# A hybrid encoder layer: the divided front weights are kept in DRAM by the first half and loaded by the second

## Chip, cores and metric

The kernel runs on one core of a Trainium2 chip. The metric is the device time of one execution in microseconds (us), given as the median of several runs. A profiled execution gives the trace; its engines are called PE (matmul), PEld (weight load for PE), DVE (vector), ACT (scalar), POOL (gpsimd) and SP (which issues DMA transfers).

## What is computed

One layer on 1024 tokens of width 1024, all in float32:

```python
p = x @ w_in[l]                                   # one projection, 43 blocks of 128 columns
y_fox  = _forgetting_attention(q, k, v, f_logit + fox_f_bias[l])
y_rwkv = _rwkv7_time_mix(r_r, r_k, r_v, ...)
merged = (sigmoid(gate_fox) * (y_fox @ p_fox[l]) + sigmoid(gate_rwkv) * (y_rwkv @ p_rwkv[l]))
x = _layer_norm(DN_ALPHA * x + merged @ w_o[l], ...)
x = _layer_norm(DN_ALPHA * x + _peer(x, peer_w_q[l], sub_keys, u, v), ...)
```

`_peer` takes, for each token, 128 experts out of 16384 (top-k over scores), a dot product with each expert's row of u, and a weighted sum of their rows of v.

## The kernel before, in words

**Exact float32 products from halves.** PE multiplies float32r operands here, so every operand is divided into a high half (a cast on ACT, line 290) and a low half (source minus high, a subtraction on POOL or DVE, line 291); `mm3` (line 283) then makes three matmuls: high by high, high by low, low by high. This holds for the activations and for the weights.

**The front, in two halves.** The tokens are processed in two halves of 512 (`PARTS`). Each half runs the forgetting attention (`fox`), the RWKV part (`rwkv_half`), the merge, the output projection with its layer norm (`merge_half`), and the query projection with its scores (`queries`). Each half reads the same list of weight tiles, 128x1024 float32 (512 KB in DRAM): 9 for the attention, 30 for RWKV and the gates, 8 for the merge, 12 for the output projection (four of them twice), 16 for the queries: 75 tiles per half, 71 different ones, 150 loads in all. `Weights` (line 294) hands them out in that order. `get` gives the pair (wh, wl) of the tile that PE is about to use. `ahead`, called just after the first matmuls of that tile, divides the next tile (ACT cast, then the subtraction, by DVE for every eighth tile and by POOL otherwise) and has SP load the raw tile after that. There are two raw buffers and two pairs. Most tiles feed 24 matmuls of 512 columns; those of the second half of the output's columns (`W_OUT` 4 to 7, each read twice) feed 12.

**Background work.** While PE goes through the front, a second stream of work is mixed in: `topk` (DVE) on the scores of finished tokens, then `experts_in`: POOL issues 128 gathers per token tile (`DMA_INDIRECT g<-u,eidx`, line 1399, 128 rows of 4 KB each), and DVE makes one dot product per gather (`CUSTOM_DVE_ANT_0 g<-g,ext`, line 1405, 1024 elements). It begins when the first half's scores are there, so it runs through the second half of the front and on into the dense block. Every matmul recorded by `mm` (line 272) gives the background some microseconds of credit, so where its steps stand among the front's depends on the matmuls alone.

**Order.** PE's order is that of the code. The orders of ACT, DVE, POOL and SP come from the framework's scheduler, which plays the program through with its own durations; each engine then takes its instructions strictly in that order. A gather on POOL waits for a free place (DVE has read it); a low half on POOL waits for the cast, which waits until PE has left the pair's buffer. SP takes its transfers in order as well: one whose buffer is not free holds up what stands behind it.

**The dense block.** After both halves, from about 1866 us, three token tiles go through all 16384 experts by matmul, and the other five by gathers of u and v.

Of the kernel before, what the change touches and what calls it, by code (L numbers as in the profile page):

```python
# [10 lines left out]
F32 = mybir.dt.float32  # L11
F32R = mybir.dt.float32r
# [35 lines left out]
LOMOD = 8  # L48
# [10 lines left out]
PARTS = [(0, 512), (512, 512)]  # L59
# [12 lines left out]
N_W = W_Q + 16  # L72
# [49 lines left out]
class Filler:  # L122


    def __init__(self):
        self.q = []
        self.debt = 0.0
# [161 lines left out]
def split(g, hi, lo, src, lo_eng=None):  # L289
    g.act.copy(hi, src)  # L290
    (lo_eng or g.dve).tensor_sub(lo, src, hi.bitcast(F32))  # L291


class Weights:


    def __init__(self, g, order):
        self.g, self.order = g, list(order)
        self.raw, self.hl = {}, {}
        self.nl = self.ns = self.n = 0  # L300
        self._load()

    def _load(self):
        if self.nl < len(self.order):
            g = self.g
            raw = g.wp.tile([128, 1024], F32, name="wraw", bufs=g.nraw)
            g.sp.dma_start(raw, g.A["w"][self.order[self.nl]])
            self.raw[self.nl] = raw
            self.nl += 1

    def _split(self):
        if self.ns < len(self.order):
            g = self.g
# [5 lines left out]
            self._load()  # L319

    def get(self, i):
        assert self.order[self.n] == i, (self.n, self.order[self.n], i)
        if self.ns <= self.n:
            self._split()
        r = self.hl.pop(self.n)
        self.n += 1
        return r

    def ahead(self):
        if self.ns <= self.n:  # L330
            self._split()


def proj_gen(g, ps, wi, x, c0, w=None, ahead=True):
# [23 lines left out]
def xload(g, hf, then=None):  # L358

    t0, n = PARTS[hf]  # L360
    g.xs = ExitStack()
    xp = g.xs.enter_context(g.tc.tile_pool(name="xp", bufs=1, side="right"))
    xh = xp.tile([128, 8, n], F32R, name="xh")
    xl = xp.tile([128, 8, n], F32R, name="xl")
    with g.tc.tile_pool(name="xr", bufs=4, side="right") as rp:
        for k in range(8):
            raw = rp.tile([128, n], F32, name="xraw")
            g.sp.dma_start(raw, g.A["xt"][k, :, t0:t0 + n])
            split(g, xh[:, k, :], xl[:, k, :], raw, g.pool if k % 3 == 2 else g.dve)
            if k == 0 and then:  # L370
                then()
    g.X = xh, xl


def body(ctx, g):
    tc, nc, A = g.tc, g.nc, g.A
    dve, act, pool, sp = g.dve, g.act, g.pool, g.sp
    cst = ctx.enter_context(tc.tile_pool(name="cst", bufs=1))
    g.lo_mod, g.nraw = LOMOD, 2
# [7 lines left out]
    def dram(name, shape, dt=F32):  # L387
        return nc.dram_tensor(name, shape, dt, kind="Internal").ap()
# [5 lines left out]
    g.gtd = [dram(f"gtd{p}", (16, 128, n)) for p, (_, n) in enumerate(PARTS)]  # L394
    g.x1d = [dram(f"x1d{t}", (128, D)) for t in range(8)]
    g.scd = [dram(f"scd{t}", (128, 2048)) for t in range(8)]
    g.cd = dram("cd", (128 * len(DENSE) // BLK, 128, 128 - HALF, BLK))
    g.yd = [dram(f"yd{t}", (128, D)) for t in range(8)]
    g.seld = [dram(f"seld{t}", (128, 128), I32) for t in range(8)]
# [23 lines left out]
    order, half = [], [FOX_F] + [FOX_QK + i for i in range(8)]  # L423
# [15 lines left out]
        order += half[:nh]  # L439
    with ExitStack() as fe:  # L440
        g.X = None
        front_setup(g, fe, order)
        for hf, (t0, n) in enumerate(PARTS):
            g.t0, g.n, g.cols = t0, n, slice(t0, t0 + n)
            with ExitStack() as hx:
                hp = hx.enter_context(tc.tile_pool(name="hp", bufs=1))
                kt = hp.tile([128, 4, n], F32, name="kt")
                more = [hp.tile([128, D], F32, name=f"g{i}") for i in range(KRING[1] if hf else 0)]
                g.keys.add(more)
                if g.X is None:  # L450
                    xload(g, hf)
                g.B.rate = RATEP[0]
                fox(g, hf, g.X)
                g.B.rate = RATEP[1]
                yr = rwkv_half(g, hf, g.X, kt) if g.stop != "fox" else None
                g.xs.close()
                g.X = None
                g.B.rate = RATEP[2]
                if g.stop not in ("fox", "rwkv"):
                    merge_half(g, hf, yr)  # L460
                g.keys.drop(more)
                g.B.busy = True
                while any(a is p for a in g.keys.alive.values() for p in more):
                    g.B._step()
                g.B.busy = False
# [20 lines left out]
def front_setup(g, fe, order):  # L486
    tc, nc, A = g.tc, g.nc, g.A
    dve, act, sp = g.dve, g.act, g.sp
    fp = fe.enter_context(tc.tile_pool(name="fe", bufs=1))
    g.wp = fe.enter_context(tc.tile_pool(name="wp", bufs=2))  # L490
    g.W = Weights(g, order)
    xload(g, 0, g.W._split)
    tab = fp.tile([128, TAB.shape[1]], F32, name="tab")
    sp.dma_start(tab, A["tab"])

    def tb(name, rows=slice(0, 128)):
        o, n = TAB_OFF[name]
        return tab[rows, o:o + n]

    g.tb = tb  # L500
    g.rst = fp.tile([128, 512], BF16, name="rst")
# [16 lines left out]
    dve.memset(g.ccar, 0.0)  # L518

def fox(g, hf, X):
# [1340 lines left out]
```

## Time and profile before

| | |
|---|---|
| median of 3 runs | 3679.65 us (3674.41 to 3681.93) |
| profiled execution, own time | 3699.46 us |
| its span from first to last instruction | 3697.7 us |
| busy: PE, DVE, POOL, ACT | 87%, 64%, 61%, 33% of the span |
| mean granted PE clock | 0.918 |
| moved by DMA | 1019 MB, mean 276 GB/s |
| casts wh and subtractions wl | 150 on ACT; 131 on POOL, 19 on DVE |
| stages (by their matmuls) | first half 6.7 to 778 us, second half 778 to 1866 us, dense block 1866 to 3698 us |

The profile's windows give the busy time of each engine in a stretch of time; its groups give the same per kind of instruction, with the idle time before them and what ended it; its waits name pairs of waiting and awaited instructions with their total time. A wait matters where it is PE's, or that of an engine for which PE waits.

### The profile page before, as it was taken

Reading aid. Unit: us, or ns where it says so; the run is one execution under the profiler, and the core shown is the slowest. Engines: PE = TensorE matmul, PEld = TensorE weight load, DVE = VectorE, ACT = ScalarE, POOL = GpSimd, SP = SyncE. Lnnn points to the kernel's source line nnn. Section 1 sums busy time; section 2 is a strip of 40 time slices with the busy share of each in tenths; the row PEclk is TensorE's granted clock in tenths of the full one; section 3 lists DMA queues with packets and bytes.
Section 4 is the critical chain, followed back from the end, with each engine's and each line's share of the span. In section 5 each row is a group of like instructions: output and inputs, shape, how many; then the busy total and the mean of one; then the engine's idle time right before and its main releaser. Section 6 shows DMA issues by size and latency. Waiting matters only on the chain. (4 is left out here: it accounts for less than half of the span.)

```text
span 3697.7 us, 55476 instructions
## 1 busy us (share of the span) xinstructions
PE 3229.0 (87%) x20656; PEld 2343.4 (63%) x20656; DVE 2367.7 (64%) x5127; ACT 1237.3 (33%) x2528; POOL 2261.5 (61%) x1752
## 2 busy tenths in 40 slices
PE   7899999989987778777867767899999999999997
PEld 5577777775565566556633322677777777776665
DVE  3235423458888998799758965577666767774324
ACT  3443222333443221222234433333333333333332
POOL 2031115426676666577845566788887888886773
PEclk9899999998988877789978889999999999999998
DMA  4121133548777777877979989999999999999995
GB/s 141 52 91 45 44 115 117 194 135 291 250 266 248 243 238 261 283 243 263 316 273 363 355 334 366 357 363 360 381 382 382 402 392 393 394 387 340 378 391 198
DMA packets 338127, 1019.35 MB, mean 276 GB/s; under 512 B 46272, under 2 KB 84928, under 8 KB 336064
## 3 DMA queue, kind: packets, MB, share of 16 engines
q0 software_dynamic: 184320, 671.17, 49.2%
q1 hardware_dynamic: 141424, 323.85, 25.0%
q10 hardware_dynamic: 12112, 20.78, 1.5%
q8 instruction: 162, 2.65, 0.3%
q14 instruction: 109, 0.89, 0.1%
HBM read 960.55 MB, written 55.12 MB: 275 GB/s over the span
## 5 line engine op out<-in xcount | busy, mean ns | idle before, releaser
L1399 POOL DMA_INDIRECT g<-u,eidx x566 | 720.0, 1272 | 350.4 <-issue 94.2
L1405 DVE CUSTOM_DVE_ANT_0 g<-g,ext 128x1024 f32<-128x1024 f32 x566 | 775.6, 1383 | 44.1 <-DMA g<-u,eidx 43.3
L291 POOL TENSOR_TENSOR wl<-wraw,wh 128x1024 fp32r<-128x1024 f32 x131 | 320.6, 2447 | 491.4 <-ACT wh L290 464.2
L1701 POOL DMA_INDIRECT vr<-v,ve x434 | 459.9, 1060 | 212.5 <-issue 106.3
L273 PE MATMUL pg<-vr,win 128*32 128x512 f32 x1736 | 314.1, 637 | 64.6 <-DMA vr<-v,ve 57.7
L273 PE MATMUL b<-xh,uh 128*128 128x384 f32 x1024 | 349.7, 341 | 13.3 <-DVE C L1586 12.1
L273 PE MATMUL b<-xh,ul 128*128 128x384 f32 x1024 | 351.1, 343 | 5.7 <-POOL ul L291 4.6
L273 PE MATMUL b<-xl,uh 128*128 128x384 f32 x1024 | 348.4, 340 | 0.0
L290 ACT CAST wh<-wraw 128x1024 fp32r<-128x1024 f32 x150 | 157.3, 1048 | 498.4 <-PE pj L273 266.0
L273 PE MATMUL v<-vl,ch 128*128 128x512 f32 x768 | 305.9, 398 | 14.0 <-POOL vl L291 13.9
L273 PE MATMUL pj<-xh,wh 128*128 128x512 f32 x624 | 291.2, 467 | 22.7 <-DVE ql L556 11.1
L273 PE MATMUL v<-vh,ch 128*128 128x512 f32 x768 | 303.1, 395 | 0.0
L273 PE MATMUL v<-vh,cl 128*128 128x512 f32 x768 | 301.7, 393 | 0.0
L290 ACT CAST uh<-uraw 128x512 fp32r<-128x512 f32 x256 | 158.5, 621 | 360.5 <-PE b L273 253.6
L273 PE MATMUL pj<-xh,wl 128*128 128x512 f32 x624 | 264.2, 423 | 5.3 <-POOL wl L291 4.1
L1701 POOL DMA_INDIRECT C<-v,ve x206 | 216.0, 1048 | 84.3 <-issue 50.0
L273 PE MATMUL pj<-xl,wh 128*128 128x512 f32 x624 | 265.0, 425 | 2.3 <-DVE xl L291 2.3
L291 DVE TENSOR_TENSOR vl<-vraw,vh 128x512 fp32r<-128x512 f32 x128 | 134.7, 1052 | 182.0 <-ACT vh L290 114.3
L290 ACT CAST vh<-vraw 128x512 fp32r<-128x512 f32 x256 | 158.1, 620 | 252.6 <-PE v L273 166.1
L273 PEld LDWEIGHTS v<-ab 128*128 128x128 f32 x768 | 114.0, 220 | 180.9 <-issue 112.4
L291 POOL TENSOR_TENSOR ul<-uraw,uh 128x512 fp32r<-128x512 f32 x128 | 171.9, 1343 | 87.3 <-ACT uh L290 71.4
L273 PEld LDWEIGHTS b<-xh,uh 128*128 128x128 f32 x1024 | 193.6, 189 | 35.1 <-DVE C L1586 16.5
(357 smaller groups left out, 6865.6 us busy)
## 6 DMA issues: line engine op xcount, KB each, us to landing
wraw<-w SPq DMA_DIRECT2D x150, 512.0 KB
uraw<-ut SPq DMA_DIRECT2D x128, 512.0 KB
vraw<-vt SPq DMA_DIRECT2D x128, 512.0 KB
cd<-S SPq DMA_DIRECT2D x12, 1344.0 KB
C<-cd SPq DMA_DIRECT2D x63, 256.0 KB
g<-u,eidx POOLq DMA_INDIRECT x566
gtd<-tmp ACTq DMA_DIRECT2D x32, 256.0 KB
g<-gtd SPq DMA_DIRECT2D x32, 256.0 KB
```

Source lines behind the costliest of these rows:

```text
L273: g.pe.matmul(o, l, r, start=start, stop=stop_)
L290: g.act.copy(hi, src)
L291: (lo_eng or g.dve).tensor_sub(lo, src, hi.bitcast(F32))
L1399: pool.indirect_dma_start(out=place, out_offset=None, in_=A["u"], in_offset=bass.IndirectOffsetOnAxis(ap=idx[:, n:n + 1], axis=0))
L1405: dve.tensor_tensor_reduce(out=gg, in0=gg, in1=xt, scale=1.0, scalar=0.0, op0=OP.mult, op1=OP.add, accum_out=hh[:, k:k + 1])
L1701: g.pool.indirect_dma_start(out=place, out_offset=None, in_=g.A["v"], in_offset=bass.IndirectOffsetOnAxis(ap=self.meta[i][1][:, t:t + 1], ...
```

## The change

The first half divides its 75 tiles as before, but each different tile's high and low half are afterwards also stored by SP to a DRAM buffer `whd` (71 tiles, two transfers of 512 KB each). The second half casts and subtracts nothing for weights: SP loads both halves from `whd` straight into a pair of tiles. The 8 KB per partition of the two raw buffers become a third pair there, so that the pair for the tile after next is asked for while a tile is in use (`_fetch`). The order of the set-up at the very start changes a little too: the first x tiles are loaded inside the half's own block, with the first division, and now the first stores, between them.

```diff
 class Weights:
-    def __init__(self, g, order):
+    def __init__(self, g, order, first):
...
+        self.pairs = [[g.wp.tile([128, 1024], F32R, name=f"w{a}{i}") for a in "hl"] for i in range(2)]
+        self.third = None
+
+    def begin(self, hf, pool):
+        if hf == 0:
+            self.raws = [pool.tile([128, 1024], F32, name=f"wraw{i}") for i in range(2)]
+            self._load()
+        else:
+            self.third = [pool.tile([128, 1024], F32R, name=f"w{a}2") for a in "hl"]
+            self.ahead()
...
+    def _fetch(self):
+        d = self.nl - self.first
+        pair = self.third if d % 3 == 1 else self.pairs[(self.first + d % 3 // 2) % 2]
+        for q in range(2):
+            self.g.sp.dma_start(pair[q].bitcast(F32), self.g.whd[self.order[self.nl], q])
+        self.hl[self.nl] = pair
+        self.nl += 1
 
     def _split(self):
-        if self.ns < len(self.order):
-            g = self.g
-            h = g.wp.tile([128, 1024], F32R, name="wh")
-            l = g.wp.tile([128, 1024], F32R, name="wl")
-            split(g, h, l, self.raw.pop(self.ns), g.pool if self.ns % g.lo_mod else g.dve)
-            self.hl[self.ns] = (h, l)
-            self.ns += 1
-            self._load()
+        g, i = self.g, self.ns
+        h, l = self.pairs[i % 2]
+        split(g, h, l, self.raw.pop(i), g.pool if i % g.lo_mod else g.dve)
+        self.hl[i] = (h, l)
+        self.ns += 1
+        self._load()
+        if self.order[i] not in self.kept:
+            self.kept.add(self.order[i])
+            for q in range(2):
+                g.sp.dma_start(g.whd[self.order[i], q], self.hl[i][q].bitcast(F32))
...
     def ahead(self):
-        if self.ns <= self.n:
+        if self.ns <= self.n and self.ns < self.first:
             self._split()
+        while self.ns == self.first and self.nl < len(self.order) and self.nl <= self.n + (self.third is not None):
+            self._fetch()
```

PE's order is the same in both programs. DVE's holds the same instructions but for the ten low halves of the second half, with small shifts between the background and the front; 384 dot products stand ahead of the dense block's first instruction in both.

**SP at the very start.** Row by row (line, operation, output<-input, shape; x4 means four in a row), SP before; `wraw` is a raw weight tile, `xraw` one of the eight x tiles of the first projection:

```order
L381 DMA base<-base 128x256
L307 DMA wraw<-w 128x1024
L368 DMA xraw<-xt 128x512
L307 DMA wraw<-w 128x1024
L368 DMA xraw<-xt 128x512 x4
L494 DMA tab<-tab 128x834
L368 DMA xraw<-xt 128x512 x3
```

and SP after:

```order
L402 DMA base<-base 128x256
L316 DMA wraw_92<-w 128x1024
L389 DMA xraw<-xt 128x512
L316 DMA wraw_93<-w 128x1024
L389 DMA xraw<-xt 128x512
L338 DMA whd<-wh_84 128x1024
L338 DMA whd<-wl_85 128x1024
L389 DMA xraw<-xt 128x512 x4
```

Two stores, which wait for the cast and the subtraction of the first weight tile, now stand ahead of six of the eight x tiles.

**POOL in the second half's output projection.** POOL before, from the merge's last addition on; `wl` is a weight's low half, `g_70<-u` a gather:

```order
L1138 TENSOR_TENSOR g_13068<-g_13068,g_13181 128x512
L291 TENSOR_TENSOR wl<-wraw,wh 128x1024
L1399 DMA g_70<-u,eidx 128x1024
L1399 DMA g_71<-u,eidx 128x1024
L1399 DMA g_72<-u,eidx 128x1024
L291 TENSOR_TENSOR wl<-wraw,wh 128x1024
L1399 DMA g_6255<-u,eidx 128x1024
```

and POOL after, from the same addition on:

```order
L1163 TENSOR_TENSOR g_12816<-g_12816,g_12921 128x512
L1424 DMA g_71<-u,eidx 128x1024
L1424 DMA g_72<-u,eidx 128x1024
L1424 DMA g_6183<-u,eidx 128x1024
L1424 DMA g_6184<-u,eidx 128x1024
L1424 DMA g_68<-u,eidx 128x1024
```

The low halves that stood between the gathers are gone, and the gathers follow one another.

**SP in the second half's queries.** SP before; `scd<-sc` stores scores, `s<-scd` reads them back for `topk`:

```order
L307 DMA wraw<-w 128x1024 x2
L1252 DMA scd<-sc 128x512 x2
L307 DMA wraw<-w 128x1024
L1252 DMA scd<-sc 128x512 x2
L1285 DMA s<-scd 128x512
L307 DMA wraw<-w 128x1024 x3
```

and SP after; `wh_84` and `wl_85`, `wh_86` and `wl_87`, `wh_6175` and `wl_6176` are the three pairs:

```order
L324 DMA wh_84<-whd 128x1024
L324 DMA wl_85<-whd 128x1024
L324 DMA wh_86<-whd 128x1024
L324 DMA wl_87<-whd 128x1024
L1277 DMA scd<-sc 128x512 x2
L1310 DMA s<-scd 128x512
L1277 DMA scd<-sc 128x512 x2
L324 DMA wh_6175<-whd 128x1024
L324 DMA wl_6176<-whd 128x1024
```

Where one raw tile was loaded, two halves are, and the stores of scores stand behind them.

More of the change, by code (lines that the diff above doesn't have):

```diff
@@ L294 @@
 class Weights:
-    def __init__(self, g, order):
-        self.g, self.order = g, list(order)
-        self.raw, self.hl = {}, {}
+    def __init__(self, g, order, first):
+        self.g, self.order, self.first = g, list(order), first
+        self.raw, self.hl, self.kept = {}, {}, set()
         self.nl = self.ns = self.n = 0
-        self._load()
+        self.pairs = [[g.wp.tile([128, 1024], F32R, name=f"w{a}{i}") for a in "hl"] for i in range(2)]
[7 more added lines that the diff above has]
+            self.ahead()
@@ L303, in _load @@
     def _load(self):
-        if self.nl < len(self.order):
-            g = self.g
-            raw = g.wp.tile([128, 1024], F32, name="wraw", bufs=g.nraw)
-            g.sp.dma_start(raw, g.A["w"][self.order[self.nl]])
+        if self.nl < self.first:
+            raw = self.raws[self.nl % 2]
+            self.g.sp.dma_start(raw, self.g.A["w"][self.order[self.nl]])
             self.raw[self.nl] = raw
             self.nl += 1
-    def _split(self):
-        if self.ns < len(self.order):
-            g = self.g
-            h = g.wp.tile([128, 1024], F32R, name="wh")
-            l = g.wp.tile([128, 1024], F32R, name="wl")
-            split(g, h, l, self.raw.pop(self.ns), g.pool if self.ns % g.lo_mod else g.dve)
-            self.hl[self.ns] = (h, l)
-            self.ns += 1
-            self._load()
+    def _fetch(self):
[5 more added lines that the diff above has]
+        self.nl += 1
@@ L321, in get @@
+    def _split(self):
+        g, i = self.g, self.ns
[8 more added lines that the diff above has]
+                g.sp.dma_start(g.whd[self.order[i], q], self.hl[i][q].bitcast(F32))
     def get(self, i):
         assert self.order[self.n] == i, (self.n, self.order[self.n], i)
-        if self.ns <= self.n:
+        if self.n < self.first and self.ns <= self.n:
@@ L329, in ahead @@
     def ahead(self):
-        if self.ns <= self.n:
+        if self.ns <= self.n and self.ns < self.first:
             self._split()
+        while self.ns == self.first and self.nl < len(self.order) and self.nl <= self.n + (self.third is not None):
+            self._fetch()
 def proj_gen(g, ps, wi, x, c0, w=None, ahead=True):
@@ L378, in body @@
     cst = ctx.enter_context(tc.tile_pool(name="cst", bufs=1))
-    g.lo_mod, g.nraw = LOMOD, 2
+    g.lo_mod = LOMOD
     base = cst.tile([128, 256], F32, name="base")
@@ L396, in body @@
     g.scd = [dram(f"scd{t}", (128, 2048)) for t in range(8)]
+    g.whd = dram("whd", (N_W, 2, 128, 1024))
     g.cd = dram("cd", (128 * len(DENSE) // BLK, 128, 128 - HALF, BLK))
@@ L441, in body @@
         g.X = None
-        front_setup(g, fe, order)
+        setup = front_setup(g, fe, order)
+        next(setup)
         for hf, (t0, n) in enumerate(PARTS):
@@ L445, in body @@
             with ExitStack() as hx:
+                g.W.begin(hf, hx.enter_context(tc.tile_pool(name="wr", bufs=1)))
                 hp = hx.enter_context(tc.tile_pool(name="hp", bufs=1))
@@ L450, in body @@
                 if g.X is None:
-                    xload(g, hf)
+                    xload(g, hf, g.W._split)
+                    next(setup)
                 g.B.rate = RATEP[0]
@@ L489, in front_setup @@
     fp = fe.enter_context(tc.tile_pool(name="fe", bufs=1))
-    g.wp = fe.enter_context(tc.tile_pool(name="wp", bufs=2))
-    g.W = Weights(g, order)
-    xload(g, 0, g.W._split)
+    g.wp = fe.enter_context(tc.tile_pool(name="wp", bufs=1))
+    g.W = Weights(g, order, len(order) // len(PARTS))
     tab = fp.tile([128, TAB.shape[1]], F32, name="tab")
-    sp.dma_start(tab, A["tab"])
     def tb(name, rows=slice(0, 128)):
@@ L500, in front_setup @@
     g.tb = tb
+    yield
+    sp.dma_start(tab, A["tab"])
     g.rst = fp.tile([128, 512], BF16, name="rst")
@@ L518, in front_setup @@
     dve.memset(g.ccar, 0.0)
+    yield
 def fox(g, hf, X):
```

## Prediction

> **What bounds the kernel now.** I read the 40 slices of the profile first: busy tenths of PE and DVE, the granted PE clock in tenths, the DMA engines' share and what they moved. A slice is 92.4 us.
>
> ```profile
> span 3697.7 us, 55476 instructions
> ...
> PE   7899999989987778777867767899999999999997
> ...
> DVE  3235423458888998799758965577666767774324
> ...
> PEclk9899999998988877789978889999999999999998
> DMA  4121133548777777877979989999999999999995
> GB/s 141 52 91 45 44 115 117 194 135 291 250 266 248 243 238 261 283 243 263 316 273 363 355 334 366 357 363 360 381 382 382 402 392 393 394 387 340 378 391 198
> ```
>
> PE is full in the first half (slices 2 to 8) and in the dense block (from slice 26). Between them, in the second half of the front, PE falls to 7 tenths, its clock to 7 or 8, and DVE stands at 8 or 9. The windows put numbers on the stages: busy time of PE, PEld, DVE, ACT and POOL, then clock, DMA share and GB/s.
>
> ```profile
> 0.00:30.00 30.00, 20.75 (x72) 14.70 (x72) 18.49 (x25) 15.82 (x21) 11.79 (x10) 1.00 0.70 232
> 584.00:666.00 82.00, 74.78 (x319) 59.87 (x318) 36.00 (x43) 22.52 (x28) 44.42 (x22) 0.96 0.42 140
> 666.00:778.00 112.00, 105.83 (x579) 90.85 (x576) 37.75 (x121) 42.17 (x67) 39.48 (x18) 1.00 0.54 183
> 778.00:1050.00 272.00, 252.30 (x1000) 155.62 (x1001) 228.24 (x643) 106.21 (x186) 150.43 (x107) 0.87 0.72 235
> 1050.00:1540.00 490.00, 381.38 (x3989) 289.51 (x3988) 442.41 (x968) 120.36 (x182) 323.11 (x234) 0.83 0.78 258
> 1584.00:1866.00 282.00, 221.08 (x977) 178.04 (x978) 234.29 (x394) 70.61 (x98) 210.61 (x129) 0.91 0.80 268
> 1866.00:3698.00 1832.00, 1631.96 (x8752) 1158.99 (x8752) 1149.22 (x2571) 666.60 (x1594) 1337.50 (x1152) 0.95 0.95 361
> ```
>
> In RWKV of the second half (1050 to 1540) DVE is busy for 442.4 of 490 us: it is the bound there, with PE in a chain with it. In merge, output projection and queries (1584 to 1866) nobody is full: PE 78%, DVE 83%, POOL 75%, DMA 0.80. PE's waits tell why, first those of 780 to 1540, then those of 1540 to 1870 (us in total, times, longest):
>
> ```profile
> PE s L273 <- DVE x L951: 31.0, 15, 4.6
> PE s L273 <- DVE Tm L961: 16.8, 7, 5.4
> PE s L273 <- DVE x L1008: 10.1, 4, 2.8
> PE pj L273 <- POOL wl L291: 4.1, 1, 4.1
> PE pj L273 <- DVE wl L291: 1.3, 1, 1.3
> ```
>
> ```profile
> PE o L273 <- POOL wl L291: 24.7, 13, 4.9
> PE o L273 <- DVE wl L291: 4.5, 1, 4.5
> PE b L273 <- POOL wl L291: 3.3, 1, 3.3
> PE a L273 <- POOL wl L291: 2.0, 1, 2.0
> PE b L273 <- DVE wl L291: 1.1, 1, 1.1
> ```
>
> In RWKV the waits are for DVE's own chain; at the end they are for the weights' low halves, 35.6 us in all.
>
> **DVE pays for POOL's subtractions.** The dot products by stage (780 to 1050, 1050 to 1540, 1540 to 1870), and their shortest, median and longest for 1050 to 1540:
>
> ```profile
> L1405 DVE CUSTOM_DVE_ANT_0 g<-g,ext 128x1024 f32<-128x1024 f32 x89 | 110.4, 1255 | 4.2 <-DMA g<-u,eidx 3.7 <-issue 0.4
> L1405 DVE CUSTOM_DVE_ANT_0 g<-g,ext 128x1024 f32<-128x1024 f32 x193 | 255.7, 1340 | 5.1 <-DMA g<-u,eidx 4.9
> L1405 DVE CUSTOM_DVE_ANT_0 g<-g,ext 128x1024 f32<-128x1024 f32 x104 | 160.7, 1563 | 27.7 <-DMA g<-u,eidx 27.5
> ```
>
> ```profile
> L1405 DVE CUSTOM_DVE_ANT_0 g<-g,ext x193: 1175/1214/4852, 1049.9 to 1539.4; 128x1024 f32<-128x1024 f32 x193
> ```
>
> The median is 1214 ns and the mean rises with the density of weight subtractions on POOL, which are these (1050 to 1540, 1540 to 1870), beside the gathers of 1050 to 1540 and DVE's own subtractions in the two stretches:
>
> ```profile
> L291 POOL TENSOR_TENSOR wl<-wraw,wh 128x1024 fp32r<-128x1024 f32 x24 | 60.7, 2527 | 10.2 <-ACT wh L290 9.9
> L291 POOL TENSOR_TENSOR wl<-wraw,wh 128x1024 fp32r<-128x1024 f32 x31 | 76.3, 2462 | 7.8 <-ACT wh L290 7.3
> L1399 POOL DMA_INDIRECT g<-u,eidx x193 | 245.6, 1273 | 144.5 <-DVE hh L1405 44.9 <-issue 28.4 <-DVE ti L1308 10.8
> L291 DVE TENSOR_TENSOR wl<-wraw,wh 128x1024 fp32r<-128x1024 f32 x4 | 4.8, 1212 | 0.0
> L291 DVE TENSOR_TENSOR wl<-wraw,wh 128x1024 fp32r<-128x1024 f32 x4 | 5.7, 1430 | 3.4 <-ACT wh L290 3.4
> ```
>
> So I read the excess over 1214 as time for which POOL's arithmetic blocks DVE. It is the main thing that the change takes away.
>
> **The change, stage by stage.** The profiled execution took 3699.46 us, 1.8 us more than its span, and lies 19.8 us (0.5%) above the median of 3679.65; I subtract from the median, as the terms are differences.
>
> *Start, +4.* Six of the eight x tiles now stand on SP behind the store of the first low half. SP issued the third x tile at once before, and DVE began the first low half at 6.0 us and needs 1.2:
>
> ```profile
> 2.60 5.62 SPq L368 DMA_DIRECT2D xraw<-xt  x4
> ```
>
> ```profile
> L291 DVE TENSOR_TENSOR wl<-wraw,wh x19: 1170/1225/2010, 6.0 to 1804.0; 128x1024 fp32r<-128x1024 f32 x19
> ```
>
> The store can go at 7.2 us, the third x tile after it instead of at about 3.0: 4.2 us later, on the path of the first projection. Less if the later x tiles waited anyway for their buffers (the row's four take until 8.2): +1; more, if the first two stores share the wire: +8.
>
> *Stores of the first half, +2.* 71 tiles times 2 x 0.524 MB are 74.4 MB. In 666 to 778 they add 16 x 1.05 MB, 150 GB/s to 183; in 584 to 666 some 15 pairs, 192 to 140. Both come to about 333, below the 402 of the fullest slice. Only the four tiles with 12 matmuls crowd: 0.52 MB read and 1.05 MB stored per 2.75 us (12 matmuls at 5.5 us per 24 in the clock-1.00 stage, an estimate from 105.83 us of PE for 16 tiles and the scores), 1.57 MB where 402 GB/s carry 1.1: 1.9 MB or 4.7 us late after four tiles, partly hidden by the next four, which store nothing. SP's waits for the low halves are nothing new: the raw load of the tile after next waited for the same subtraction. Behind a waiting store stand raw loads, score stores and reads, needed a tile later. Bounds 0 and +16 (1 us per query tile).
>
> *778 to 1050, -4.* 89 x (1255 - 1214) ns is 3.6 us of DVE, and some casts leave ACT. PE is 93% busy, so hardly more; bounds 0 and -9.
>
> *1050 to 1540, -21.* 193 x (1340 - 1214) ns is 24.3 us. POOL's arithmetic there is 323.1 - 245.6 = 77.5 us, of which the weights are 60.7, so I give them 78%: 19.0. With DVE's four own subtractions, 4.8, DVE is spared 23.8 us; DVE is on the path for 442.4/490 = 0.90 of the stage: 21. Bounds: only the 5.4 us of waits for low halves; or all of 24.3 + 4.8 + 5.4 = 34.
>
> *1584 to 1866, -20.* Here 35.6 us of waits for low halves go, and 104 x (1563 - 1214) = 36 us of DVE are eased. But something is late next: the transfers. The stage moves 282 x 268 = 75.6 MB; 36 tiles at another 0.524 MB make 94.5. At the dense block's mean of 361 GB/s this takes 262 us: -20, which I take, because that row is a long stretch in which gathers and weights run together as here. At 402 it would take 235 us: -47. If transfers give everything back: 0. The cover is the third pair: a tile is asked for two tiles ahead, about 11 us in the query stage, and 1.05 MB take 2.9 us at 361 GB/s; the four short tiles, passed twice, use up 1.05 MB per 2.75 us and will wait.
>
> [...]
>
> *Dense block, 0.* PE's order is the same, and 384 dot products stand ahead of it on DVE in both orders, so it starts with the same work left; bounds -5 and +5.
>
> Sum: +4 + 2 - 4 - 21 - 20 = -39 us, 3679.65 - 39 = 3641. With the lower ends 3586 (+1 + 0 - 9 - 34 - 47 - 5 = -94), with the upper 3704 (+8 + 16 + 0 - 5 + 0 + 5 = +24). About 0.2%, 7.4 us, is what can be told from no change.
>
> **Rivals.**
>
> *Late weights (slower).* In 1540 to 1870 raw tiles of half a megabyte already came late although asked for a tile ahead:
>
> ```profile
> ACT wh L290 <- DMA wraw<-w: 16.9, 5, 4.8
> ```
>
> Now a tile is a megabyte, and up to seven gathers stand in the engines beside it. If two in three of the 36 pairs come 3.4 us late (16.9/5), PE waits 82 us where it waited 35.6: +46 in that stage, in all +4 + 2 - 4 - 21 + 46 = +27, 3707. It decides from 1.5 us per pair on: 36 x 1.5 = 55 us, 19 more than now, eats the other 19. For it: share 0.80 before 25% more bytes. Against: the two tiles of lead, and a queue that shares evenly still gives 36 x 1.05 MB / 201 GB/s (half of 402) = 188 us in a stage of 282. Chance 0.16.
>
> *Pace of the first half (much faster).* The first matrix product of the two merges:
>
> ```profile
> L273 PE MATMUL a<-xh,wh x64: 387/389/796, 562.8 to 1627.6; 128*128 128x512 f32 x64
> ```
>
> The same merge, output and query code as here took from that first start, 562.8, to 778 in the first half, 215 us, with the clock at 0.96 to 1.00, against 282 here at 0.91. If the low halves' waits held PE back twice, by themselves and through the clock, the stage gains up to the 47 of 402 GB/s, RWKV its 34, the first half costs 1 and 778 to 1050 gives 9: -89, 3591. [...] Against: DVE stays near 85%. Chance 0.17.
>
> *Nothing on the path (no change).* The eased DVE time turns into waits for PE or for gathers (27.5 us of DVE's idle time is that already), so RWKV gives 5 and the last stage 5: +4 + 2 - 0 - 5 - 5 = -4, 3676. Against: PE waits 57.9 us for DVE's x and Tm in RWKV, so DVE is on the path. Chance 0.11.
>
> **How the numbers follow.** The sum has 0.56 and by itself reaches from 3615 to 3670 (a gain of half its 45 us with a dear first half, or of one and a half times). Faster by over 0.2%: 0.56 + 0.17 = 0.73; within: 0.11; slower: 0.16. The range 3592 to 3682 holds the sum, no change and most of the fast rival; it leaves out nearly all of the slow one and a little below, about 0.2.
>
> **What would show it.** Right: dot products at a mean of about 1.24 us in 1050 to 1540 and under 1.35 in the last stage, 64 subtractions fewer on POOL, RWKV of the second half some 20 us shorter, the last stage near 262 us at about 360 GB/s, the first half ending near 784 us, the dense block again 1832 us. Wrong: dot products still at 1.34 (then something else blocks DVE); PE waits for DMA into wh or wl above 55 us (the slow rival); a last stage at 282 without such waits (no change); a first half beyond 795 us.

## The result, and the profile after

Median 3629.97 us over 6 runs (3624.21 to 3650.85), beside 3680.79 for the kernel before in the same measurement: a ratio of 0.9862, 95% interval 0.9842 to 0.9883, which is 51 us less. Measured once more at the end, on another chip, the ratio was 0.9885 (0.9863 to 0.9907), 42 us less. 3641 had been forecast, 39 less. The total came out about right; most of its terms did not, as the stages show.

The profiled execution after (3650.85 us, 21 above its median, as that of before was 20 above its own): busy tenths, clock and GB/s of the 40 slices.

```profile
span 3649.1 us, 55730 instructions
...
PE   7899998899997877788766867999999999999997
...
DVE  2234423347978998887468955677666767763324
...
PEclk9899999997988988889878989999999999999998
...
GB/s 213 108 237 119 93 186 235 275 305 199 327 262 379 285 251 308 357 326 377 322 325 352 361 354 376 349 356 367 382 388 372 403 389 393 398 383 342 385 387 193
```

The ninth slice, mostly still the first half, now moves 305 GB/s, where it moved 135. Windows give the stages, in the columns used before: the output projection of the first half, RWKV of the second half with its gates, then merge, output projection and queries of the second half.

```profile
614.00:677.50 63.50, 52.69 (x193) 41.00 (x194) 17.08 (x23) 12.43 (x14) 24.83 (x11) 0.85 0.62 223
1067.10:1551.60 484.50, 383.88 (x4138) 288.62 (x4137) 429.75 (x1047) 105.28 (x174) 279.79 (x231) 0.87 0.88 322
1551.60:1822.00 270.40, 215.44 (x977) 175.07 (x978) 182.08 (x389) 36.72 (x63) 116.19 (x98) 0.90 0.90 345
```

The same places before, cut at the same matmuls (the output projection, RWKV, the last stage):

```profile
613.90:664.30 50.40, 47.38 (x192) 37.22 (x191) 18.78 (x24) 12.78 (x14) 23.25 (x10) 0.95 0.37 124
1050.00:1584.60 534.60, 413.79 (x4137) 308.37 (x4135) 473.09 (x1045) 134.00 (x205) 348.70 (x253) 0.81 0.78 258
1584.60:1866.20 281.60, 221.28 (x978) 178.24 (x979) 233.69 (x393) 70.01 (x97) 210.11 (x129) 0.91 0.79 268
```

RWKV with its gates fell from 534.6 to 484.5 us, 50 less; DVE is busy 43.3 us less in it. The prediction's term ends at 1540, before the gates. That stretch alone, before and after, cut at the same matmuls:

```profile
1050.00:1540.30 490.30, 381.68 (x3989) 289.76 (x3988) 442.71 (x968) 120.36 (x182) 323.11 (x234) 0.83 0.78 258
```

```profile
1067.10:1516.90 449.80, 360.19 (x3990) 274.78 (x3990) 399.48 (x968) 92.68 (x152) 254.31 (x211) 0.87 0.87 315
```

It fell by 40.5 us, where 21 had been expected. The gates behind it, 44.3 us before and 34.7 after, had no term; DVE is as busy in them as before (30.4 and 30.3 us). The last stage fell by 11, not 20. The output projection of the first half, which should have cost next to nothing, takes 13 us more.

PE executes the same 20656 matmuls in the same order in every kernel of this study, so a stage can be cut in each trace at the same numbered matmuls. These are the times between those matmuls' starts, in us, in one profiled execution each. "Start" is the first 28.6 us of before, from the first matmul at 6.7 us on; the next column is the rest of the first half up to the merge; merge, output projection and queries are those of the first half; "to 1050" is the second half up to RWKV; "RWKV" includes the gates; "last" is the second half's merge, output projection and queries; "dense" runs to the last matmul's end.

| kernel | start | to 563 | merge | output | queries | to 1050 | RWKV | last | dense |
|---|---|---|---|---|---|---|---|---|---|
| before | 28.6 | 527.5 | 51.1 | 50.4 | 114.2 | 271.5 | 534.6 | 281.5 | 1809.1 |
| after | 33.2 | 519.6 | 55.0 | 62.9 | 116.5 | 273.2 | 484.4 | 270.5 | 1804.8 |
| stores only (e1) | 33.0 | 528.2 | 55.9 | 56.9 | 114.6 | 269.4 | 525.4 | 280.9 | 1799.6 |
| subtractions kept (e2) | 32.8 | 522.4 | 54.0 | 61.1 | 116.9 | 258.0 | 535.7 | 314.2 | 1786.0 |
| casts kept (e3) | 32.4 | 527.9 | 54.4 | 62.4 | 118.1 | 266.0 | 494.1 | 294.3 | 1801.3 |
| low halves only (e4) | 29.8 | 523.4 | 50.8 | 62.0 | 118.9 | 258.1 | 494.3 | 297.0 | 1801.6 |
| one subtraction moved (e5) | 33.7 | 527.8 | 55.7 | 64.7 | 114.3 | 269.6 | 490.2 | 266.8 | 1803.6 |
| low halves, two raw (e6) | 29.6 | 520.5 | 50.9 | 62.0 | 119.0 | 261.5 | 497.1 | 264.3 | 1802.6 |
| subtractions on DVE (e7) | 27.8 | 527.4 | 50.9 | 50.3 | 114.2 | 261.3 | 511.3 | 270.7 | 1796.7 |
| two pairs (e8) | 33.2 | 527.3 | 55.3 | 62.5 | 116.4 | 249.1 | 491.3 | 295.5 | 1805.7 |
| stores off SP (e9) | 32.7 | 524.2 | 52.3 | 53.6 | 125.0 | 263.3 | 470.8 | 266.3 | 1774.1 |
| scores off SP (e10) | 32.6 | 520.2 | 55.6 | 58.3 | 121.3 | 258.8 | 473.2 | 261.4 | 1775.9 |
| after again (e11) | 33.4 | 522.7 | 55.5 | 61.4 | 114.2 | 259.3 | 474.1 | 263.5 | 1773.0 |
| together (e12) | 32.3 | 525.2 | 53.1 | 53.3 | 126.8 | 264.5 | 473.5 | 260.5 | 1777.5 |

Two columns show how far a single execution can be trusted. "To 1050" scatters from 249 to 273 us with no visible relation to what a kernel does there. The dense block is the same work everywhere and takes 1786 to 1809 in most runs, but 1773 to 1778 in the last four, which ran on two faster chips (there the kernel before has medians of 3640 and 3642, elsewhere 3675 to 3681). So a kernel's time is told below as a ratio to the kernel before on its own chip, with its 95% interval, and RWKV and last stage of e9 to e12 stand beside each other only.

**What DVE lost to POOL.** RWKV's dot products after, then two of the smallest of DVE's operations there, before and after (columns: count, total us, mean ns):

```profile
L1430 DVE CUSTOM_DVE_ANT_0 g<-g,ext 128x1024 f32<-128x1024 f32 x194 | 237.9, 1239 | 20.2 <-DMA g<-u,eidx 15.8 <-issue 4.0
```

```profile
L766 DVE SCALAR_TENSOR_TENSOR kt<-prev,vec,tmp 128x1 f32<-128x1 f32 x4 | 6.2, 1548 | 0.0
L766 DVE SCALAR_TENSOR_TENSOR rt<-prev,vec,tmp 128x1 f32<-128x1 f32 x4 | 6.1, 1532 | 0.0
```

```profile
L791 DVE SCALAR_TENSOR_TENSOR rt<-prev,vec,tmp 128x1 f32<-128x1 f32 x4 | 0.9, 221 | 0.0
L791 DVE SCALAR_TENSOR_TENSOR kt<-prev,vec,tmp 128x1 f32<-128x1 f32 x4 | 0.8, 208 | 0.0
```

Of DVE's 43.3 us the dot products are 17.8 (255.7 - 237.9, with the stage cut at 1540 as in the prediction) and its own four subtractions 4.8, both as forecast. The other 20.7 are operations on which no term had been set. The plainest are those above: one element per partition, 0.2 us of work, 1.5 us before. The timelines of DVE and POOL before show one of them:

```profile
1068.72 0.74 DVE L765 SCALAR_TENSOR_TENSOR kt<-pj,vec,tmp 128x511 f32<-128x511 f32 x1
1069.38 1.69 DVE L766 SCALAR_TENSOR_TENSOR kt<-prev,vec,tmp 128x1 f32<-128x1 f32 x1
1071.00 0.41 DVE L1360 TENSOR_TENSOR s<-s 128x512 bf16<-128x512 bf16 x1
```

```profile
1068.49 2.56 POOL L291 TENSOR_TENSOR wl<-wraw,wh 128x1024 fp32r<-128x1024 f32 x1
```

The small operation starts at 1069.38 and ends at 1071.07; POOL's subtraction ends at 1071.05. DVE had 0.2 us of work and stood still until POOL was done. The operation ahead of it, which takes one of its inputs from a matmul's output (`pj`), ran beside the same subtraction in 0.74 us. So do the others of its kind: of the twelve operations `kt`, `rt` and `vt` from `prev` before, seven met a weight's subtraction on POOL, took 1.7 to 2.6 us and ended within 0.03 us after it; the other five met none and took 0.2. After, all twelve take 0.2 to 0.3 us.

### The profile page after: what moved, and what is told of

Same layout as the page of the kernel before. It is cut to its first block, busy times and chain, and to the rows that moved or that the text cites. A ratio compares the mean times of both kernels' runs of the same rounds, so it can differ in the third digit from the quotient of the medians.

```text
span 3649.1 us, 55730 instructions
## 1 busy us (share of the span) xinstructions
PE 3189.5 (87%) x20656; PEld 2319.2 (64%) x20656; DVE 2251.3 (62%) x5118; ACT 1164.7 (32%) x2453; POOL 2060.3 (56%) x1686
## 5 line engine op out<-in xcount | busy, mean ns | idle before, releaser
L1424 POOL DMA_INDIRECT g<-u,eidx x566 | 689.4, 1218 | 491.5 <-DVE hh L1430 171.4
L1430 DVE CUSTOM_DVE_ANT_0 g<-g,ext 128x1024 f32<-128x1024 f32 x566 | 725.6, 1291 | 72.5 <-DMA g<-u,eidx 63.4
L291 POOL TENSOR_TENSOR wl<-wraw,wh 128x1024 fp32r<-128x1024 f32 x65 | 155.6, 2393 | 460.6 <-ACT wh L290 445.1
L273 PEld LDWEIGHTS b<-xh,ul 128*128 128x128 f32 x1024 | 192.6, 188 | 35.0 <-issue 25.1
```

Source lines behind the costliest of these rows:

```text
L273: g.pe.matmul(o, l, r, start=start, stop=stop_)
L1424: pool.indirect_dma_start(out=place, out_offset=None, in_=A["u"], in_offset=bass.IndirectOffsetOnAxis(ap=idx[:, n:n + 1], axis=0))
L1430: dve.tensor_tensor_reduce(out=gg, in0=gg, in1=xt, scale=1.0, scalar=0.0, op0=OP.mult, op1=OP.add, accum_out=hh[:, k:k + 1])
```

## The experiments

**e1, the stores alone.** The kernel before, with this added to its `_split`:

```diff
+            i = self.order[self.ns - 1]
+            if self.ns <= len(self.order) // 2 and i not in self.kept:
+                self.kept.add(i)
+                for q, t in enumerate((h, l)):
+                    g.sp.dma_start(g.whd[i, q], t.bitcast(F32))
```

> The kernel before, with one part of the change alone: each of the 71 distinct weight tiles of the first half is stored (high and low half) to DRAM; the second half still loads the raw tiles and divides them, and reads nothing of what was stored. Theory (from the two profiles: PE at the end of the first half stands 15.4 us later after the change, 12.8 of it in the output projection): the stores alone cost 12 to 18 us, and the time is about 3695 against 3680 before. Rival (the term of the prediction, +2 for the stores and +4 for the start): the difference of the two profiles is one execution's, and the stores cost about 6 us: 3686. A second rival: the second half makes the delay good again because DVE, not PE, bounds it: under 4 us.

Measured: 1.0045 (1.0027 to 1.0063), 16.5 us slower. The theory held for the total: the stores cost 10 to 23 us, and the second half of the change must therefore earn about 67, not 51. In its trace the output projection of the first half loses 6.5 us, not 12.8, and the merge 4.8. In that output projection PE waits for a store:

```profile
PE o L273 <- DMA whd<-wh: 6.2, 1, 6.2
```

A pair is free for the tile after next only when its stores have been read out of it; the short tiles leave about 2.75 us for that (an estimate: 12 matmuls, one every 0.23 us). RWKV of this kernel, 525.4, is the second witness of the kernel before (534.6).

**e2 and e3, one engine's work put back.** The second half loads one raw buffer and one stored half, and computes the other half; bytes per tile as in the change. Its core, for the subtractions (e2); for e3 the line is `g.act.copy(h, raw)`, and the low half is fetched:

```diff
-        for q in range(2):
-            self.g.sp.dma_start(pair[q].bitcast(F32), self.g.whd[self.order[self.nl], q])
+        self.g.sp.dma_start(pair[0].bitcast(F32), self.g.whd[self.order[i], 0])
...
+            raw = self.raw.pop(i)
+            (g.pool if i % g.lo_mod else g.dve).tensor_sub(l, raw, h.bitcast(F32))
```

> The change, but the second half loads the raw tile and the stored high half, and POOL (DVE for every eighth tile) subtracts again; no casts. The bytes per tile are the same as in the change. Theory: the subtractions on POOL are what costs DVE its time in RWKV (dot products 18 us, its own subtractions 5, other operations of DVE 21 us). With them back, RWKV of the second half takes about 530 us again instead of 485, and the whole 3680 to 3695 (the stores' 15 us are paid, the gain of 50 in RWKV and some of the last stage are gone). Rival A: POOL's queue, where a subtraction waited for its cast and the gathers waited behind it (events on POOL 28 us before, 4 after): there is no cast to wait for any more, so half of the gain stays: about 3655. Rival B: the gain is the weights' earlier arrival (three buffers instead of two), not the arithmetic: within 10 us of the change, 3625 to 3640.

> The change, but the second half loads the raw tile and the stored low half, and ACT casts the high half again; no subtractions. The bytes per tile are the same as in the change. Theory (the subtractions are what costs): within 8 us of the change, 3622 to 3638. Rival: the chain raw tile, cast, matmul delays PE as before (ACT was 24 to 26 per cent busy in the second half, and its cast waits for PE to leave the buffer): half of the gain gone, about 3655.

Measured: e2 1.0126 (1.0099 to 1.0154), 46 us slower, at 3722 beyond the 3680 to 3695 expected; e3 1.0009 (0.9993 to 1.0025), none of the change's gain. The total of e3 spoke against the theory, the stages for it. RWKV: 535.7 with the subtractions, 494.1 with the casts. e2 in RWKV, its window, its dot products and POOL's subtractions:

```profile
1052.10:1587.80 535.70, 412.79 (x4138) 310.16 (x4136) 475.15 (x1051) 105.44 (x174) 348.32 (x256) 0.80 0.83 289
```

```profile
L1439 DVE CUSTOM_DVE_ANT_0 g<-g,ext 128x1024 f32<-128x1024 f32 x195 | 259.8, 1345 | 8.9 <-DMA g<-u,eidx 8.7 <-issue 0.2
L338 POOL TENSOR_TENSOR wl<-wraw,wh 128x1024 fp32r<-128x1024 f32 x24 | 61.8, 2574 | 26.8 <-DMA wraw<-w 11.8 <-issue 6.7 <-DVE hh L1447 4.4
```

As many bytes as in the change, no casts, the high halves fetched early, and DVE is as busy as before (475 against 473), its dot products at 1345 ns (1340): the subtractions on POOL are the cost, and what else the change does buys next to nothing in RWKV. Nor is it the single raw buffer of these two kernels, since e3 has it as well. What both lost, they lost in the last stage (314 and 294 us), for a reason of their own: that one raw buffer. For e3 the run e6 below shows it; for e2 it is only argued. PE waits there in e3, and SP:

```profile
PE o L273 <- ACT wh L338: 38.1, 13, 5.9
```

```profile
SPq L318 <- DMA wraw<-w: 90.3, 21, 10.5
```

**e4, low halves only,** as the second half of e3 reads no stored high half:

```diff
-            for q in range(2):
+            for q in (1,):
                 g.sp.dma_start(g.whd[self.order[i], q], self.hl[i][q].bitcast(F32))
```

> As the run that keeps the casts, and the first half stores only the low halves (37 MB instead of 74), as the second half reads no stored high half. Theory: the stores' cost in the first half comes from the crowd of 1.57 MB for each short tile of the output projection; with 1.05 MB it goes down by 8 to 12 us: 3615 to 3625, the fastest yet. Rival: the cost is that SP's queue waits in front of each store for a subtraction, which stays: no faster than the run that keeps the casts.

Measured: 0.9973 (0.9950 to 0.9997), 14 us under e3 on the same chip: more than the 8 to 12 of the theory, though far from its 3615 to 3625. In the traces the start (29.8 against 32.4) and the merge (50.8 against 54.4) are cheaper, 6 us; the rest of the 14 lies in stretches that scatter. The output projection, where the theory had placed the gain, still takes 62.0 us: half the bytes, the same loss. So the crowd of bytes on the wire (the DMA engines' throughput), as the prediction had it, fell as the reason there. For the whole kernel the halved stores do count; whether by their bytes or by their places on SP, which were halved with them, this run does not tell.

**e5, one subtraction moved.** In all four traces so far PE waited in that output projection for a low half that DVE did behind layer norm:

```diff
-        split(g, h, l, self.raw.pop(i), g.pool if i % g.lo_mod else g.dve)
+        split(g, h, l, self.raw.pop(i), g.pool if i % g.lo_mod or i == 56 else g.dve)
```

> The change, but one subtraction of the first half, that of the tenth tile of the output projection (every eighth one is DVE's), goes to POOL instead. In the profiles of the change and of the three variants before, with half the stores too, PE loses 12 us or so in the first half's output projection, and there DVE does this subtraction only behind 6 us of layer norm, while the kernel before did it in the middle of them. Theory: it is the scheduler's order, not the stored bytes: without this subtraction on DVE the output projection of the first half loses 3 to 6 us instead of 12.8, and the time is 55 to 60 us under the kernel before (the change itself: 50). Rival: the short tiles' 1.57 MB each are what is late: the loss stays at 10 to 13, and the time is 48 to 52 under the kernel before.

Measured: 0.9874 (0.9853 to 0.9894), and the output projection takes 64.7 us. The theory fell; 14.3 us are lost there, a little more than the rival's 10 to 13, and the whole is 46 us under before. PE's waits there, then SP's:

```profile
PE o L273 <- POOL wl L291: 7.6, 5, 2.4
PE o L273 <- ACT wh L290: 5.5, 2, 4.8
PE o L273 <- DMA whd<-wh: 5.4, 1, 5.4
```

```profile
SPq L338 <- ACT wh L290: 18.8, 5, 10.3
SPq L338 <- POOL wl L291: 13.2, 7, 2.1
SPq L1196 <- DVE x L1245: 9.5, 2, 6.6
```

The waits only changed their names. SP stands for 41 us of the 65 at stores of halves (L338) and of the layer norm's x (L1196), with the next raw tiles behind them. That SP stands is not new: before, it stood for nearly all of the stage, mostly at raw loads that waited for low halves (43.9 us). New are the stores ahead of the raw loads.

**e6, a second raw buffer for e4** from the merge on, where there is room:

```diff
+    def second(self, pool):
+        if self.third is not None:
+            self.raws[1], self.more = pool.tile([128, 1024], F32, name="wraw2"), True
...
+        g.W.second(lp)
```

> As the run that stores only the low halves and casts again, but with a second raw buffer from the merge of the second half on (there is room from there). That run gained 53 us in RWKV and gave about 34 back in the output projection and the queries. Theory: it gave them back because the next raw tile could only be asked for after the cast had emptied the one buffer; with two, the last stages are as in the change, and as the first half costs 3 to 4 less, the time is 50 to 60 us under the kernel before. Rival: the chain raw tile, cast, matmul is late by itself in the last stages: 10 to 30 under.

Measured: 0.9879 (0.9856 to 0.9903), 45 us under before, the change's own size but short of the 50 to 60 expected; the last stage takes 264.3 us instead of 297.0. Its theory held for the stage. (Of the 53 us that its expectation gives to RWKV in e4, 13 lie in "to 1050", which scatters.) So casting again costs nothing that the total shows once a raw tile can be asked for early, and only the low halves have to be kept.

**e7, the subtractions on DVE.** One line in the kernel before, no DRAM:

```diff
-            split(g, h, l, self.raw.pop(self.ns), g.pool if self.ns % g.lo_mod else g.dve)
+            split(g, h, l, self.raw.pop(self.ns), g.pool if self.ns % g.lo_mod and self.ns < len(self.order) // 2 else g.dve)
```

> The kernel before, nothing stored or fetched; but all 75 subtractions of the second half are DVE's (1.2 us each), none POOL's. Theory: one of POOL's subtractions costs DVE more than to do it itself, as DVE stands still for most of the 2.5 us: in RWKV 24 x 1.2 = 29 us more against 18 + 21 us less, in the last stage 33 more against some 40 less: 5 to 20 us under the kernel before. Rival: POOL's subtractions mostly run beside DVE, and DVE, the bound of RWKV, gets 64 x 1.2 = 77 us more: 30 to 60 us over the kernel before.

Measured: 0.9904 (0.9881 to 0.9928), 35 us under before, more than the theory's 5 to 20, and three quarters of the change. RWKV takes 511.3 us; dot products and DVE's subtractions in it:

```profile
L1405 DVE CUSTOM_DVE_ANT_0 g<-g,ext 128x1024 f32<-128x1024 f32 x194 | 234.4, 1224 | 8.2 <-DMA g<-u,eidx 7.4 <-issue 0.8
L291 DVE TENSOR_TENSOR wl<-wraw,wh 128x1024 fp32r<-128x1024 f32 x28 | 34.4, 1230 | 1.3 <-ACT wh L290 1.3
```

DVE, the bound of this stage, takes 24 more subtractions upon itself, 29.6 us, and is still busy 12 us less than before (461.2 against 473.1).

**e8, two pairs:**

```diff
-        pair = self.third if d % 3 == 1 else self.pairs[(self.first + d % 3 // 2) % 2]
+        pair = self.pairs[self.nl % 2]
...
+        if self.n not in self.hl:
+            self._fetch()
...
-        while self.ns == self.first and self.nl < len(self.order) and self.nl <= self.n + (self.third is not None):
+        while self.ns == self.first and self.nl < len(self.order) and self.nl <= self.n:
```

> The change without the third pair: both halves of a tile are asked for one tile ahead, in two pairs. Theory (the third pair is the cover of the last stage, and RWKV does not need it, as its gain comes from the subtractions): RWKV of the second half keeps its gain of 40 to 50 us, the last stage loses 20 to 40 against the change, as a pair of 1.05 MB has only the 2.75 us of a short tile to arrive: 10 to 30 under the kernel before. Rival A: the third pair does nothing: 45 to 50 under. Rival B: RWKV needs it too: at or over the kernel before.

Measured: 0.9937 (0.9922 to 0.9953), 24 us under before, as the theory had it: RWKV 491.3 keeps its gain, the last stage takes 295.5. PE's waits there, of this kernel and of the change:

```profile
PE o L273 <- DMA wh<-whd: 31.8, 9, 10.1
PE o L273 <- DMA wl<-whd: 14.6, 8, 4.6
```

```profile
PE o L273 <- DMA wh<-whd: 19.0, 4, 9.2
PE o L273 <- DMA wl<-whd: 9.0, 7, 2.1
```

The third pair is worth some 25 us in that stage (18 to 27 by the totals, on different chips). But three pairs still leave 28 us of waits, one of 9.2.

**e9, the stores off SP:**

```diff
             for q in range(2):
-                g.sp.dma_start(g.whd[self.order[i], q], self.hl[i][q].bitcast(F32))
+                e = (g.pool if i % g.lo_mod else g.sp) if q else g.act
+                e.dma_start(g.whd[self.order[i], q], self.hl[i][q].bitcast(F32))
```

> The change, with the same bytes stored, but not by SP: ACT issues the store of a high half behind its own cast, POOL that of a low half behind its own subtraction (SP only where DVE subtracts). Moving one subtraction did not cure the first half's output projection (14.8 us lost instead of 12.8), so the theory that this subtraction's place on DVE costs it has fallen. New theory: SP takes its transfers in order, and the raw tiles stand behind stores that wait for casts, subtractions and (x1d) the layer norm; in the profile of the change SP stands 9.6 us for the layer norm's x with the next raw tile behind it. With the stores off SP, SP's queue in the first half is that of the kernel before: the start loses under 2 us, the output projection under 5, the first half ends within 6 us of the kernel before instead of 15 to 24, and the time is 58 to 66 us under the kernel before. Rival: the wire is full (1.57 MB per short tile): the loss stays at 10 or more, 45 to 52 under.

Measured: 0.9846 (0.9822 to 0.9870), 56 us under before, short of the 58 to 66 expected, and its interval overlaps with the change's. The output projection does come back, to 53.6 us (50.4 before), as the theory said. But the start still loses 4.1 us, where under 2 had been expected, and the queries behind the output projection take 125.0 instead of 114: the first half still ends 16 us late (at 794.5, against 778.5 before and 794.0 in the change). In the queries ACT waits:

```profile
ACT sc L1277 <- DMA scd<-sc: 27.9, 4, 11.9
```

ACT's copies of the scores wait until earlier scores have landed in DRAM, and the cast of the next weight tile stands behind them; PE then waits 2.6 us for it. The same wait of ACT was 20.6 us before, but its longest was 6.2. For the wait of 11.9 SP had issued two stores of scores behind two raw tiles, from 712.0 on; ACT's copy, which waited for the first of them to land, started at 722.55, 10.5 us later, and from 700 to 720 all traffic together was 326 GB/s at a DMA share of 0.90. Whether SP's order or the traffic made it late, no run tells apart. The loss moved on; it did not go: merge, output projection and queries together take 230.9 us here and 231.1 in the change's second execution (e11).

**e10, the stores of the scores off SP.** What stood behind what in the queries of the second half, on SP's timeline of the change, and SP's wait there:

```profile
1717.34 0.38 SPq L324 DMA_DIRECT2D wl<-whd  x1
1718.66 1.21 SPq L1277 DMA_DIRECT2D scd<-sc  x2
1733.04 0.32 SPq L1310 DMA_DIRECT2D s<-scd  x1
1733.69 2.21 SPq L1277 DMA_DIRECT2D scd<-sc  x2
1735.99 0.41 SPq L324 DMA_DIRECT2D wh<-whd  x1
```

```profile
SPq L1310 <- DMA scd<-sc: 13.1, 1, 13.1
```

From 1718.7 to 1736.0 SP asks for no weights, 13.1 us of it at a read of scores whose own store has not landed; the fetches behind it then come 9.2 us late for PE. The transfers were not idle meanwhile. The window of that stretch has a DMA share of 1.03 and 412 GB/s, more than the fullest slice:

```profile
1718.70:1736.00 17.30, 17.30 (x87) 14.64 (x87) 8.52 (x15) 2.21 (x5) 6.04 (x7) 1.00 1.03 412
```

```diff
-                sp.dma_start(g.scd[tt0 + tt][:, gr * 512:(gr + 1) * 512], sc)
+                act.dma_start(g.scd[tt0 + tt][:, gr * 512:(gr + 1) * 512], sc)
```

> The change, but the stores of the scores (16 in each half, 256 KB each) are issued by ACT, behind its own copy of the scores, instead of by SP. In the profile of the change SP stood twice, 13.1 and 9.4 us, at a read of scores that waited for the landing of their store, which went out behind fetched weights in the same queue; three fetched tiles stood behind that read, and PE then waited 9.2 and 5.4 us for a high half. Theory: late weights in the queries come from this place in SP's order and not from the wire: with it gone those two waits shrink to under 6 us together, and the time is 6 to 10 us shorter than the change, 56 to 62 under the kernel before. Rival: the wire is what makes scores and weights late: 46 to 52 under, and PE waits as long for the halves.

Measured: 0.9861 (0.9835 to 0.9886), the change's own ratio; 51 us under is the rival's total (46 to 52). PE's waits in the last stage:

```profile
PE o L273 <- DMA wl<-whd: 10.0, 7, 2.9
PE o L273 <- ACT q L1289: 8.9, 1, 8.9
...
PE o L273 <- DMA wh<-whd: 4.6, 3, 2.9
```

The waits for high halves fell from 19.0 (18.8 in e9, on the same chip) to 4.6, so SP's order does decide where PE waits for them. But PE now waits 8.9 us for a copy on ACT, and the stage is only 5 us shorter than in e9 (261.4 against 266.3). The rows speak for the theory, the total for the rival: as the wire was full as well, the run does not part them.

**e11 and e12, the change again, and all together:** the stores as in e9, the scores as in e10, and a fourth pair of tiles from the merge of the second half on.

> The change itself once more, beside the next kernel on the same chip. Expected: 46 to 54 us under the kernel before, as the first time (ratio 0.9862).

> The change with what the runs pointed to: the stores of the halves issued by ACT and POOL, the stores of the scores by ACT, and a fourth pair of tiles in the second half from the merge on (there is room from there). Theory (what the change gives back, it gives back to SP's order): the first half's output projection loses 4 instead of 13, and the waits for halves in the second half's output projection and queries, 28 us in the change, fall under 15: 60 to 70 us under the kernel before, clear of the change. Rival: waits that PE does not lose to the halves it loses to ACT and POOL, which now stand at transfers: 48 to 58 under, not clear of the change.

Measured on one chip: the change 0.9885 (0.9863 to 0.9907), e12 0.9844 (0.9815 to 0.9872). The change came out 4 us short of what was expected. e12 has the lower median, 3590.87 against 3597.28, but the intervals overlap: whether it beats the change is not settled, and its size fits the rival (48 to 58 under; it is 57). The output projection loses 2.9 us and the waits for halves in the last stage are down to 5.9, as its theory had it, but the queries of the first half take 126.8. Its longest wait in the last stage is again ACT's:

```profile
PE o L273 <- ACT q L1299: 15.4, 1, 15.4
```

## Why the prediction was right, and where it was not

That the sum came near is luck. Two of its terms were too small, with opposite signs: the stores of the first half cost some 15 us more than forecast, RWKV up to 1540 earned some 20 more. The last stage earned 9 less, and two stretches without a term, 29 to 563 and the gates, came out 7.9 and 9.6 us shorter, no more than they scatter from kernel to kernel (519.6 to 528.2, and 34.7 to 44.3). Of the signs that the prediction named, the dot products came as said (1239 ns, and 1265 in the last stage); the first half, at 794 us, ended just short of the 795 that was to count against it.

- *Start, +4:* 4.6 measured, and 3.7 to 5.1 in every kernel that stores both halves, none without stores (e7). SP's rows came as computed: the store of the first low half at 7.4 us, the third x tile right behind it. But that order is not the whole cause. e4 and e9 have the same order on SP, with two x tiles more ahead of that store; e4, which stores no high halves, loses 1.2 us, e9 still 4.1.
- *Stores of the first half, +2:* this step failed. With merge, output projection and queries taken together (215.7 us before), the change loses 18.7, its second execution 15.4, e1 11.7; e1's own ratio puts start and stores at 16.5 together where 6 had been forecast. The argument was "Only the four tiles with 12 matmuls crowd", a matter of megabytes, and "SP's waits for the low halves are nothing new". Half the megabytes cost as much in the output projection (e4, e6). What was new there was that each pair is held until its stores have read it (PE waits of 6.2 us in e1, 5.4 in e5), and that SP, in order, puts raw tiles behind more waits; take the stores off SP, and the output projection nearly comes back (e9). But the queries then lose as much again, and halving the stores took 14 us off the whole kernel (e4 against e3). How the 15 us by which the first half ends late divide between order and bytes stays open.
- *778 to 1050, -4:* not to be told; the stage scatters by 24 us from kernel to kernel.
- *1050 to 1540, -21:* right in mechanism, half its size. This stretch gained 40.5 us against the profile of before and 37 against e1. Dot products (19.0 expected, 17.8) and DVE's own subtractions (4.8, 4.8) came as computed. Missing was a term for DVE's other operations, 20.7 us: the mean of one group had been read for the excess, and the groups whose minimum and mean lie as far apart had not been looked at. The rows of 1.5 us for one element per partition stood in the trace of before. e2 (535.7 us in RWKV) and e7 (511.3) show that it is POOL's subtractions; e3 (494.1) and e8 (491.3), that neither casts nor lead matter much there.
- *1584 to 1866, -20:* 11 less in the first profile (10.4 against e1). The 35.6 us of waits for low halves went, the transfers came next, and the stage moves 270.4 us x 345 GB/s = 93.3 MB where 94.5 had been expected. The rate was mis-sized: 345 GB/s, where 361 had been taken. And 28 us of waits for fetched halves came in the place of the old ones, the longest of them behind a read of scores at which SP stood while the wire was full (e10). "The cover is the third pair" held: without it 295.5 us (e8).
- *Dense block, 0:* 1809.1 to 1804.8, while e1, with the same work in it, has 1799.6: nothing.
- *Rivals.* Late weights: PE waited 28 us for halves, under the 55 named; but two pairs (46 us and more) or one raw buffer (e3, with the total of the kernel before) show how near it lay. Pace of the first half: the last stage's clock stayed (0.90 against 0.91). Nothing on the path: RWKV refutes it.

## What to carry to other kernels

Where DVE bounds a stage, as RWKV here, count a subtraction on POOL at the price of the DVE time that it blocks: a 128x1024 one, 2.5 us on POOL, blocked some 1.6 us of DVE here ((17.8 + 20.7)/24). DVE did it itself in 1.2, and one line (e7) earned 35 us where a round trip through DRAM earned 42 to 51. Look for such blocking in the smallest operations: those of one element per partition took 0.2 us alone and 1.7 to 2.6 beside a subtraction. When transfers are added to a queue that is taken in order, price the waits that they stand in as well as their bytes (in e5 SP stood for 41 of 65 us), and look at the read that waits for its own store: what was asked for early stood behind it, for 13.1 us in the change.

## What the runs showed of the hardware

Two short waits of PE, 2.8 us together, were followed by 5.7 us at a granted clock of 0.50, in which the matmuls lost another 2.6 us. PE in the first half's output projection of the change (start, duration, in brackets the wait ahead):

```profile
647.42 0.39 PE L273 MATMUL o<-wh,ml 128*128 128x512 f32 x1
648.73 0.50 PE L273 MATMUL o<-wh,mh 128*128 128x512 f32 x1 [0.92 <-ACT wh L290]
651.16 0.79 PE L273 MATMUL o<-wl,mh 128*128 128x512 f32 x1 [1.92 <-POOL wl L291]
651.75 0.63 PE L273 MATMUL o<-wh,ml 128*128 128x512 f32 x1
...
656.87 0.48 PE L273 MATMUL o<-wh,ml 128*128 128x512 f32 x1
657.19 0.39 PE L273 MATMUL o<-wh,mh 128*128 128x512 f32 x1
```

The window from 652 to 656 has the granted clock of that time, 0.50:

```profile
652.00:656.00 4.00, 4.00 (x10) 3.05 (x10) 0.69 (x1) 0.51 (x1) 2.38 (x1) 0.50 0.80 260
```

After two waits of 0.92 and 1.92 us with a single matmul between them, a matmul takes 0.63 us instead of 0.39 for some 5.7 us, until 656.9; they start every 0.43 us instead of every 0.23, so the 13 of them lose another 2.6 us. Single waits of 1.3 us (648.9 before) and 1.4 us (606.1 in the change) were followed by no such stretch; one of 6.3 us (666.5 in the change) was: 9 matmuls start every 0.44 us, at a clock of 0.50, until 670.5. How long a wait it takes, these rows do not tell. This is why the output projection takes 12.5 us longer while the waits within it, 10.9 us against 3.0 before, are only 7.9 longer: the slower matmuls behind these two waits (2.6 us) and behind that of 6.3 us (9 x 0.21, some 1.9 us) make up nearly all of the rest.
